# Eight sums of the out projection's weight, beside the first columns of the second half's input projection instead of beside that half's local attention

## The chip, the cores and the metric

The kernel runs on one core of a Trainium2 chip. The metric is device time in microseconds: 2577.95 us before the change, the median of three runs (2577.09 to 2580.97). The chip has other cores, and nothing runs on them here. The engines are called as in the profile: PE (matrix multiplication) with PEld (its weight loads), DVE (vector), ACT (scalar), POOL (GpSimd), and SP, which only issues transfers here. Each engine takes its own instructions strictly in the order of its queue.

## What is computed

One layer of a sequence model over 2048 tokens of width 1024, in float32:

```python
u = rms_norm(h, g_mix_pre)
z = u @ w_in                                   # 1024 x 2816
ya = swa_with_sinks(qa, ka, va, sinks)         # local attention, 8 heads of 64
yh = hgrn2(qh, fh, ih, gh, lb, onorm)          # gated linear recurrence, 4 heads of 128
y = concatenate([ya, yh]) @ w_out              # the out projection
h = h + rms_norm(y, g_mix_post)
...                                            # cross attention, then a SwiGLU block
```

The change touches only when four combinations of the blocks of `w_out` (1024 x 1024) are computed. It changes no value.

## The kernel before, in words

**Precision.** A float32 product is made of three fast products: each operand is split into a rounded high part (`hi`) and the rest (`lo`), and PE multiplies high by high, high by low and low by high (`mm3`, lines 166 to 168; `products`, lines 1047 to 1049). The split of a 128x1024 tile costs one pass of POOL or ACT for `hi` (line 146 or 148) and one of DVE for `lo` (line 149).

**Seven products for eight.** The large products are done in 2x2 blocks with seven block products (Strassen's scheme in Winograd's form). The side that stays in memory, here the weight, is needed in seven forms: three of its four blocks as they are, and four combinations of blocks, called 5, 7, 6 and 4 in the code. With blocks a(i,j) of the weight these are, each made from the one before: 5 = a(0,1) - a(0,0), 7 = a(1,1) - a(0,1), 6 = 7 + a(0,0), 4 = a(1,0) - 6.

**Where the combinations of `w_out` are made.** `combined` (lines 951 to 971) makes them ahead of time, in two halves of 128x1024 elements each, and so issues eight sums. One sum is: the load of one or two tiles of `w_out` on SP's queue (line 75; tile `x`), three steps of waiting (`yield`), one `TENSOR_TENSOR` of DVE (line 958, `x<-x,x`), the store of the result to the DRAM tensor `w_s` on SP's queue (line 78), and one more `yield`. A half takes 16 steps of the generator. The blocks a(0,j) are loaded in two transfers of 64 partitions each, the blocks a(1,j) in one. In all that is 20 loads (16 of 256 KB, 4 of 512 KB), 8 sums and 8 stores of 512 KB. Much later the out projection loads `w_s` and splits it (lines 911 and 914).

The tag `x` has three buffers. It is also the tile of the decays of the input projection (line 652: `e1`), once for each of four pairs of columns, and of the folded weights of the cross attention later.

**The stages around the change** (`mix`, lines 202 to 270). First comes the input projection of tokens 0 to 1023 in seven-product form (`in_first`). Then a stage of four interleaved generators:

- `in_proj(1, u)`, called `cols`: the input projection of tokens 1024 to 2047, column by column. A column has 128 outputs; its weights are loaded (tile `raw`, three buffers) and split (`whi`, `wlo`), and PE multiplies 2 x 24 products of 128x512. The first step takes two columns (keys and values of the local attention), each later one takes one; there are 21 steps.
- `swa(range(8))`: local attention of the first half, one step for each 128 tokens, and one more.
- `hgrn(range(8))`: the recurrence of the first half.
- `swa(range(8, 16))`: local attention of the second half.

The order of the text is: two steps of `cols`; then per step of the first half's local attention five steps of the recurrence and one of `cols`; then per step of the second half's local attention one step of `cols` and, from the second on, four steps of the sums, which is one sum. The last sum stands beside the last step.

**What sets the real order.** The text only gives a priority. A scheduler, run when the program is built, walks through a model of the engines and gives each engine, whenever it comes free, the first instruction in the order of the text whose inputs and buffers are there. So a load whose buffer is free is put early in SP's queue, whatever the text has beside it. The result is one fixed queue for each engine. On the chip an instruction at the head of a queue that waits holds up all behind it.

`mark` (lines 982 to 987) notes the last ACT and DVE instruction of the text so far, and `behind` (lines 974 to 980) makes the DVE sums of line 958 stand behind it in DVE's queue. Loads and stores are not bound by it.

**Memory.** The pools of this stage reuse the room of those of `in_first`. As the pools are laid out, one of the three `x` buffers lies in room that no tile had before; the two others lie where the tile `pair` of the last load `pair<-un_d` was. Its last reader is the split of that tile by DVE (line 914, `u<-pair`).

Of the kernel before, what the change touches and what calls it, by code (L numbers as in the profile page):

```python
# [28 lines left out]
NPB = TB // P  # L29
NT = T // P  # L30
# [18 lines left out]
class Layer:  # L49
# [152 lines left out]
    def mix(self):  # L202
        tc, I = self.tc, self.I
        kw = dict(reuse_waits="tile")
        with contextlib.ExitStack() as left:
            def pool(name, at, **k):
                return at.enter_context(tc.tile_pool(name=name, bufs=1, **k, **kw))

            self.mc = pool("mc", left)
            self.r_x = self.cst.tile([P, NT], F32, name="r_x")  # L210
            with (
                tc.tile_pool(name="t1", bufs=3, **kw) as self.ts,
                tc.tile_pool(name="t2", bufs=3, **kw) as self.tb,
                tc.tile_pool(name="s1", bufs=2, side="right", **kw) as self.st_pool,
                contextlib.ExitStack() as at,
            ):
                self.banks(at, "ps1", **MOST)
                self.raws, self.parts, self.sums = 3, 3, 3
                u = self.in_first()
            self.banks(left, "ps2", **FOUR)  # L220
            self.hg = pool("hg", left)
            self.wp = pool("wp", left)
            self.io = pool("io", left)
            with tc.tile_pool(name="sw", bufs=1, side="right", **kw) as self.sw:
                self.zero_tiles()
                swa = self.swa(range(NPB), "st")
                hgrn = self.hgrn(range(NPB), "h")
                cols = self.in_proj(1, u)
                for _ in range(2):
                    next(cols)  # L230
                for _ in swa:
                    for _ in range(5):
                        next(hgrn)
                    next(cols)
                for _ in hgrn:
                    pass
                jobs = self.jobs()
                sums = self.w_sums()
                swa = self.swa(range(NPB, NT), "sth")
                for i, _ in enumerate(swa):  # L240
                    next(cols)
                    if i:
                        self.mark()
                        for _ in range(4):
                            next(sums, None)
                for _ in cols:
                    pass
                for _ in sums:
                    pass
            phases = self.phases(jobs, None, lambda: self.io_tile("z"))  # L250
            with tc.tile_pool(name="xp", bufs=1, side="right", **kw) as self.xp:
                fold = self.fold_cross()
                for i, _ in enumerate(self.hgrn(range(NPB, NT), "gt")):
                    for _ in range(1 if i % 5 else 0):
                        next(fold)
                for _ in range(8):
                    next(phases)
                for _ in fold:
                    pass
            left.close()  # L260
            with (
                tc.tile_pool(name="t3", bufs=3, **kw) as self.ts,
                tc.tile_pool(name="t4", bufs=3, **kw) as self.tb,
                tc.tile_pool(name="s3", bufs=2, side="right", **kw) as self.st_pool,
                contextlib.ExitStack() as at,
            ):
                self.banks(at, "ps3", **MOST)
                self.raws, self.parts, self.sums = 6, 4, 5
                for _ in phases:
                    pass  # L270
# [1437 lines left out]
```

## Time and profile before

| what | value |
|---|---|
| median of three runs | 2577.95 us |
| the profiled execution's own time | 2576.83 us |
| its span, first to last instruction | 2574.7 us |
| granted TensorE clock, mean | 0.995 |
| stage of the change, roughly | 260 to 660 us of the span |
| sums of line 958, first and last start | 524.2 and 636.7 us |
| first load of `w_out` for them | 504.2 us |
| first and last store to `w_s` | 525.5 and 638.0 us |
| first load of `w_s` by the out projection | 664.8 us |

In the rows that follow, `x` and a number in brackets is a count of instructions; in the table by windows each engine's busy time in microseconds stands ahead of its count, then the granted clock of PE, the mean busy share of the 16 DMA engines, and GB/s. Times on a timeline are microseconds from the start of the span, followed by the duration; `[4.91 <-DMA x<-in_w_out_dram]` says that the engine stood idle for 4.91 us before the instruction and what ended that.

### The profile page before, as it was taken

How to read it: one execution, taken by the hardware profiler on the slowest of the kernel's cores; microseconds unless marked ns; L12 is line 12 of the kernel's file. 1: busy time of each engine (PE TensorE's matmuls, PEld its weight loads, DVE VectorE, ACT ScalarE, POOL GpSimd, SP SyncE). 2: the span in 40 equal slices, each digit the busy share in tenths (PEclk: the TensorE clock that was granted, in tenths of full speed). 3: DMA queues.
4: the chain of work that ended last, by engine and by line, in shares of the span. 5: the costliest groups of instructions: out<-in, count | busy, mean ns of one | idle time of the engine just before them, and what ended most of it. 6: DMA issues, size and time to landing. Idle time of an engine off the chain costs nothing.

```text
span 2574.7 us, 34494 instructions
## 1 busy us (share of the span) xinstructions
PE 2518.1 (98%) x12160; PEld 2108.6 (82%) x12160; DVE 1747.3 (68%) x2781; ACT 1262.3 (49%) x2641; POOL 481.6 (19%) x651
## 2 busy tenths in 40 slices
PE   7989999999999999999999999999999999999998
PEld 6878788878997888888788888888888888888786
DVE  7675578778666668697776665575666566664756
ACT  5453366656555575565564333353333334543443
POOL 4240334321321334224210000000000000000022
PEclk9999999999999999999999999999999999999999
DMA  5335655484896787767983542253555434576798
GB/s 188 135 119 180 198 159 153 150 259 169 251 331 236 229 273 218 246 229 207 314 264 123 171 163 83 82 196 123 180 200 193 158 128 142 191 220 185 224 222 211
DMA packets 285389, 495.78 MB, mean 193 GB/s; under 512 B 20640, under 2 KB 143520, under 8 KB 285216
## 3 DMA queue, kind: packets, MB, share of 16 engines
q1 hardware_dynamic: 272256, 446.38, 51.5%
q0 software_dynamic: 10656, 38.80, 8.1%
q10 hardware_dynamic: 2304, 8.39, 0.8%
q8 instruction: 96, 1.57, 0.3%
q14 instruction: 77, 0.63, 0.1%
HBM read 326.78 MB, written 166.72 MB: 192 GB/s over the span
## 4 chain that ended last, share of the span: by engine, by line
PE 86%; DMA 5%; DVE 4%; issue 2%; POOL 2%; ACT 1%; SPq 0%; DVEq 0%; POOLq 0%; ACTq 0%
PE psm L1047 23%; PE psm L1049 23%; PE psm L1048 23%; PE psg L168 2%; PE psg L166 2%; PE psg L167 2%; PE pss L1299 2%; DMA pair<-in_x_dram 1%; PE pss L167 0%; PE psh L168 0%; PE psh L167 0%; PE pss L168 0%; PE pss L166 0%; PE psh L166 0%; DMA qd<-z_d 0%
## 5 line engine op out<-in xcount | busy, mean ns | idle before, releaser
L1047 PE MATMUL psm<-T,S 128*128 128x512 f32 x2664 | 1032.7, 392 | 14.9 <-ACT part L1062 8.6
L1048 PE MATMUL psm<-T,S 128*128 128x512 f32 x2664 | 1039.5, 390 | 0.0
L1049 PE MATMUL psm<-T,S 128*128 128x512 f32 x2664 | 1033.6, 391 | 2.2 <-DVE S L914 2.2
L1047 PEld LDWEIGHTS psm<-T,S 128*128 128x128 f32 x2664 | 501.1, 188 | 121.9 <-ACT part L1062 10.5
L1049 PEld LDWEIGHTS psm<-T,S 128*128 128x128 f32 x2664 | 500.9, 188 | 108.2 <-DVE S L914 4.4
L1048 PEld LDWEIGHTS psm<-T,S 128*128 128x128 f32 x2664 | 501.2, 188 | 102.6
L911 ACT ACTIVATE S<-sum 128x512 fp32r<-128x512 f32 (+1 forms) x338 | 207.9, 619 | 329.6 <-PE psm L1049 320.5
L914 DVE TENSOR_TENSOR S<-sraw,S 128x512 fp32r<-128x512 f32 (+1 forms) x311 | 214.8, 698 | 220.6 <-ACT S L911 208.3
L914 DVE TENSOR_TENSOR S<-sum,S 128x512 fp32r<-128x512 f32 (+1 forms) x404 | 277.1, 691 | 79.9 <-ACT S L911 67.0
L1062 ACT ACTIVATE part<-psm 128x512 f32<-128x512 f32 x297 | 175.3, 592 | 188.9 <-PE psm L1049 180.5
L911 ACT ACTIVATE S<-sraw 128x512 fp32r<-128x512 f32 (+1 forms) x272 | 166.4, 617 | 143.3 <-PE psm L1049 137.6
L1417 POOL DMA_DIRECT2D row<-y_d x28 | 25.0, 892 | 1071.4 <-DMA sraw<-hid_d 905.3
L1388 ACT ACTIVATE junk<-row 128x512 f32<-128x512 f32 x160 | 99.6, 624 | 95.3 <-DVE row L1410 34.6
L914 DVE TENSOR_TENSOR T<-row,T 128x1024 fp32r<-128x1024 f32 x104 | 123.3, 1193 | 29.6 <-ACT T L911 29.3
L166 PE MATMUL psg<-u,whi 128*128 128x512 f32 x352 | 141.8, 403 | 1.0 <-POOL whi L148 1.0
L168 PE MATMUL psg<-u,wlo 128*128 128x512 f32 x352 | 140.2, 398 | 1.5 <-DVE wlo L149 1.5
L167 PE MATMUL psg<-u,whi 128*128 128x512 f32 x352 | 140.1, 398 | 0.0
L911 ACT ACTIVATE T<-row 128x1024 fp32r<-128x1024 f32 x104 | 105.6, 1026 | 24.7 <-DMA row<-in_w_down_dram 11.8
L913 POOL TENSOR_SCALAR S<-sum 128x512 fp32r<-128x512 f32 x66 | 51.9, 787 | 217.8 <-PE psm L1049 138.6
L1592 DVE TENSOR_TENSOR part<-psm,part 128x512 f32<-128x512 f32 x66 | 45.5, 689 | 66.5 <-PE psm L1049 66.4
L149 DVE TENSOR_TENSOR wlo<-raw,whi 128x1024 fp32r<-128x1024 f32 x54 | 68.8, 1274 | 27.6 <-ACT whi L146 18.9
L1583 DVE TENSOR_TENSOR row<-psm,part 128x512 f32<-128x512 f32 x66 | 45.5, 690 | 56.0 <-PE psm L1049 55.7
(331 smaller groups left out, 3659.2 us busy)
## 6 DMA issues: line engine op xcount, KB each, us to landing
sraw<-in_w_gate_dram SPq DMA_DIRECT2D x44, 512.0 KB, 4.9
sraw<-in_w_up_dram SPq DMA_DIRECT2D x44, 512.0 KB, 4.8
hid_d<-row SPq DMA_DIRECT2D x44, 512.0 KB, 2.7
h_d<-row SPq DMA_DIRECT2D x32, 512.0 KB, 6.9
y_d<-row SPq DMA_DIRECT2D x32, 512.0 KB, 3.8
sraw<-hid_d SPq DMA_DIRECT2D x32, 512.0 KB, 5.2
row<-h_d POOLq DMA_DIRECT2D x30, 512.0 KB, 7.7
row<-y_d POOLq DMA_DIRECT2D x28, 512.0 KB, 7.2
```

Of the source, the lines that this page charges most:

```text
L149: nc.vector.tensor_tensor(lo, raw, f32(hi), ALU.subtract)
L166: nc.tensor.matmul(ps, ah, bh, start=(i == 0), stop=False)
L167: nc.tensor.matmul(ps, ah, bl, start=False, stop=False)
L168: nc.tensor.matmul(ps, al, bh, start=False, stop=(i == n - 1))
L911: self.nc.scalar.activation(hi, raw, AF.Copy)
L913: self.nc.gpsimd.tensor_scalar(hi, raw, 1.0, 1.0, ALU.mult, ALU.mult)
L914: self.nc.vector.tensor_tensor(lo, raw, f32(hi), ALU.subtract)
L1047: nc.tensor.matmul(ps, s[:, 0, k, :], t[:, 0, k, :], start=st, stop=False, **kw)
L1048: nc.tensor.matmul(ps, s[:, 0, k, :], t[:, 1, k, :], start=False, stop=False, **kw)
L1049: nc.tensor.matmul(ps, s[:, 1, k, :], t[:, 0, k, :], start=False, stop=sp, **kw)
L1062: nc.scalar.activation(t, ps, AF.Copy)
L1388: self.nc.scalar.activation(junk, a, AF.Square, scale=float(D) ** -0.5, accum_out=to)
```

## The change

The creation of the sums' generator (and of `jobs`, which issues nothing by itself) moves ahead of the two first steps of `cols`. Each of these two steps is now followed by 16 steps of the sums, which is one whole half, four sums. The loop over the second half's local attention loses its sums.

```diff
                 cols = self.in_proj(1, u)
+                jobs = self.jobs()
+                sums = self.w_sums()
                 for _ in range(2):
                     next(cols)
+                    self.mark()
+                    for _ in range(16):
+                        next(sums, None)
+                for _ in sums:
+                    pass
                 for _ in swa:
                     for _ in range(5):
                         next(hgrn)
                     next(cols)
                 for _ in hgrn:
                     pass
-                jobs = self.jobs()
-                sums = self.w_sums()
-                swa = self.swa(range(NPB, NT), "sth")
-                for i, _ in enumerate(swa):
+                for _ in self.swa(range(NPB, NT), "sth"):
                     next(cols)
-                    if i:
-                        self.mark()
-                        for _ in range(4):
-                            next(sums, None)
                 for _ in cols:
-                    pass
-                for _ in sums:
                     pass
```

The same 20 loads, 8 sums and 8 stores are issued, by the same engines and queues. In the text they stand ahead of all local attention and all of the recurrence, behind three of the 22 columns. The `mark` of the first four sums now names the second column's last instructions, that of the last four the third column's.

## The prediction

> **What bounds the kernel now.** The page comes first: its span, its engine totals and the chain that ended last.
>
> ```profile
> span 2574.7 us, 34494 instructions
> PE 2518.1 (98%) x12160; PEld 2108.6 (82%) x12160; DVE 1747.3 (68%) x2781; ACT 1262.3 (49%) x2641; POOL 481.6 (19%) x651
> PE 86%; DMA 5%; DVE 4%; issue 2%; POOL 2%; ACT 1%; SPq 0%; DVEq 0%; POOLq 0%; ACTq 0%
> ```
>
> PE is busy for 98% of the span, 2574.7 - 2518.1 = 56.6 us short of all of it. The change adds and removes no matmul, so it can only win or lose pieces of such idle time. The next question is where they lie. The table by windows of 10 us answers it (columns: PE, PEld, DVE, ACT, POOL, clock, DMA share, GB/s); first the place that the sums go to, then the place that they leave, then the seam to the next stage.
>
> ```profile
> 260.00:270.00 10.00, 6.99 (x25) 4.82 (x24) 9.27 (x11) 5.55 (x7) 5.85 (x6) 0.90 0.88 279
> 270.00:280.00 10.00, 10.00 (x43) 8.24 (x43) 6.70 (x10) 0.91 (x3) 8.61 (x8) 0.93 0.92 314
> 280.00:290.00 10.00, 10.00 (x45) 8.26 (x45) 3.03 (x4) 2.41 (x4) 1.81 (x2) 1.00 0.53 155
> 290.00:300.00 10.00, 10.00 (x46) 8.27 (x45) 1.23 (x1) 1.20 (x2) 1.05 (x1) 1.00 0.47 167
> 300.00:310.00 10.00, 10.00 (x57) 8.68 (x56) 5.73 (x26) 5.61 (x23) 2.37 (x3) 1.00 0.50 154
> 310.00:320.00 10.00, 10.00 (x60) 8.74 (x59) 5.15 (x18) 2.64 (x7) 3.88 (x7) 1.00 0.62 184
> 320.00:330.00 10.00, 10.00 (x52) 8.42 (x52) 9.31 (x25) 7.32 (x25) 3.21 (x6) 1.00 0.42 135
> ...
> 530.00:540.00 10.00, 9.52 (x48) 7.69 (x46) 4.89 (x9) 3.25 (x9) 2.05 (x3) 1.00 1.06 302
> 540.00:550.00 10.00, 7.91 (x38) 6.00 (x39) 9.09 (x24) 5.17 (x15) 6.05 (x9) 1.00 0.93 299
> 550.00:560.00 10.00, 8.11 (x47) 6.76 (x46) 6.60 (x16) 3.37 (x10) 1.26 (x2) 1.00 1.05 310
> ...
> 650.00:660.00 10.00, 7.18 (x37) 5.91 (x37) 7.34 (x12) 4.20 (x9) 2.12 (x3) 0.85 1.02 329
> 660.00:670.00 10.00, 9.09 (x71) 8.64 (x71) 6.49 (x12) 6.88 (x19) 6.27 (x7) 0.97 1.04 295
> ```
>
> Three windows beside the sums, 530 to 560, lose 0.48 + 2.09 + 1.89 = 4.46 us of PE, with the DMA engines full. From 270 to 330 PE loses nothing, and between 280 and 300 DVE is all but idle. The seam at 650 to 670 loses 2.82 + 0.91 = 3.73 us.
>
> Is the loss at 530 to 560 caused by the sums? The view of the tile `x` over 500 to 640 us, the timeline of DVE, and that of PE say so:
>
> ```profile
> L75 SPq DMA_DIRECT2D x<-in_w_out_dram x20: 390/606/1635, 504.2 to 604.2; - x20
> L958 DVE TENSOR_TENSOR x<-x,x x8: 1210/1226/1239, 524.2 to 636.7; 128x1024 f32<-128x1024 f32 x8
> L78 SPq DMA_DIRECT2D w_s<-x x8: 320/334/490, 525.5 to 638.0; - x8
>   DMA x<-in_w_out_dram: 4.9, 1
>   issue: 3.4, 1
>   DMA w_s<-x: 0.9, 1
> ```
>
> ```profile
> 536.63 1.23 DVE L958 TENSOR_TENSOR x<-x,x 128x1024 f32<-128x1024 f32 x1 [4.91 <-DMA x<-in_w_out_dram]
> 543.39 1.23 DVE L958 TENSOR_TENSOR x<-x,x 128x1024 f32<-128x1024 f32 x1 [0.85 <-DMA w_s<-x]
> 557.18 1.23 DVE L958 TENSOR_TENSOR x<-x,x 128x1024 f32<-128x1024 f32 x1 [3.36 <-issue]
> ```
>
> ```profile
> 540.59 0.66 PE L760 MATMUL pss<-ident,S 128*128 128x128 f32 x4 [1.07 <-DVE w_mn L731]
> 547.93 0.50 PE L769 MATMUL psh<-pth,vst 128*128 128x512 f32 x1 [1.19 <-ACT pth L764]
> 558.82 0.63 PE L760 MATMUL pss<-ident,S 128*128 128x128 f32 x4 [1.90 <-DVE vst L712]
> ```
>
> A sum stands at the head of DVE's queue and waits for its load or for a buffer; the local attention's DVE work behind it is late; PE waits 1.07, 1.19 and 1.90 us for that work or what follows from it. The three waits of the sums add to 9.1 us, of which about half reaches PE.
>
> **The change part by part.** *Taken away from 504 to 638 us:* 20 loads, 8 sums (8 x 1.226 = 9.8 us of DVE) and 8 stores. DVE and SP have no say of their own in the end here; what the path gets back is the 4.46 us of PE. Bounds: 0, if another wait steps in (a `qd` load that is late anyway), and 4.46 from those windows. I take the upper end: PE reads 10.00 in the windows on both sides where DVE isn't held by a sum. What is late next there is the local attention's own chain, which the rows of 270 to 330 show to be covered in the first half by the same kind of columns.
>
> *Put at 260 to 350 us:* the same 48 instructions. On DVE the sums stand behind the split of the second and third column, and PE has those columns' products to do meanwhile:
>
> ```profile
> 269.73 2.06 DVE L149 TENSOR_TENSOR wlo<-raw,whi 128x1024 fp32r<-128x1024 f32 x1
> 271.71 2.06 DVE L914 TENSOR_TENSOR u<-pair,u 128x1024 fp32r<-128x1024 f32 x1
> 273.69 1.63 DVE L149 TENSOR_TENSOR wlo<-raw,whi 128x1024 fp32r<-128x1024 f32 x1
> 287.27 1.23 DVE L149 TENSOR_TENSOR wlo<-raw,whi 128x1024 fp32r<-128x1024 f32 x1 [1.06 <-POOL whi L148]
> ...
> 303.19 0.35 DVE L731 CUSTOM_DVE_ANT_0 S<-pst,wmask,nsink 128x128 f32<-128x128 f32 x1 [9.19 <-PE pst L727]
> ```
>
> Two of the three `x` buffers come free when the last `u<-pair` ends (271.71 + 2.06 = 273.8). No sum can run before one of them is loaded, and by then the three columns are split (273.69 + 1.63 = 275.3). Their 3 x 48 = 144 products at 45 to 46 per 10 us keep PE for about 32 us, to near 298. DVE's first work for the local attention is at 303.19, where DVE, not PE, has waited 9.19 us. So the first sums fall into a time in which nobody waits for DVE.
>
> Not all eight do. The DMA view gives their transfers:
>
> ```profile
> x<-in_w_out_dram SPq DMA_DIRECT2D x16, 256.0 KB, 6.4
> x<-in_w_out_dram SPq DMA_DIRECT2D x4, 512.0 KB, 5.9
> w_s<-x SPq DMA_DIRECT2D x8, 512.0 KB, 4.7
> qd<-z_d SPq DMA_DIRECT2D x64, 128.0 KB, 3.3
> ```
>
> 16 x 256 + 4 x 512 + 8 x 512 KB are 10.5 MB, 34 us of all DMA engines at the 302 to 314 GB/s of the full windows. The share left free from 270 to 330 is 0.08 + 0.47 + 0.53 + 0.50 + 0.38 + 0.58 = 2.54 windows, 25 us. So the sums end near 350, and about a third of them stand beside the first local attention of the first half, with the DMA engines as full as at 530 to 560. Bounds of their cost there: 0, as in the full window 270 to 280, and 4.46 us in 30 us over the 50 us from 300 to 350, 7.4 us. I take 1.5 us: the rate of 0.149 us per us over one window, 320 to 330, the only one of the six after 270 whose DVE is nearly full (9.31), since a held DVE harms only where it has no slack.
>
> The Trainium skill speaks against this change at this point (page DMA: Bandwidth & Descriptors, section "Issuing engines are not separate DMA queues"): all transfers end on the same 16 DMA engines and interleave there, whichever engine issued them. By it the sums' bytes crowd the loads of whatever stage they are put in. The trace agrees with the rule where it shows it, with a share of 1.06, 0.93 and 1.05 at 530 to 560. By it alone the sum would be the first rival's, below.
>
> *SP's queue.* The 28 issues move past all loads of the first half's local attention and recurrence; a store waits for its sum, a load for its buffer, and behind each stand loads of `qd`, `kr`, `raw`. At 0.3 to 0.6 us an issue they are about 14 us of SP over 80 us, no bound. What such a wait can do is the second rival.
>
> *The earliest load.* One `x` buffer lies in unused room, so its first 512 KB may be loaded far ahead, as the gain of the memory tokens was:
>
> ```profile
> L75 SPq DMA_DIRECT2D g<-in_g_mem_dram x1: 328/328/328, 161.7 to 161.7; - x1
> ```
>
> It was loaded at 161.7 us, as its buffer came free, for work near 580. Such a load costs 0 to 1.7 us (0.52 MB at 302 GB/s) if it crowds the start of the kernel; I take 0, by the nearest row: in the window 270 to 280, at a DMA share of 0.92, PE loses nothing.
>
> *The seam.* It may win all of its 3.73 us or lose as much again; the instructions there are the same, so I take 0.
>
> **Sum.** -4.46 + 1.5 = -2.96 us on the profiled execution, whose own time is 2576.83 us with a span of 2574.7: 2573.9. The median of the runs is 1.12 us above that execution: 2577.95 - 2.96 = **2575.0 us**.
>
> **The rivals.**
>
> *The crowd only moves.* The sums cost at 300 to 350 what they cost at 530 to 560, 4.46 us: 2577.95 us. For it speaks the sum of bytes; against it DVE's slack. This is also the case in which the change doesn't do what it says: the text sets a priority only, and if the scheduler puts most sums behind 300 us, they stand beside a local attention again.
>
> *Slower, by SP's and DVE's queues in the first half.* Each sum that reaches the head of DVE's queue too early holds DVE, and its store holds SP, as at 536.63, for 4.91 us. DVE's idle time from 280 to 320 is 6.97 + 8.77 + 4.27 + 4.85 = 24.9 us; less 9.8 us for the sums, 15.1 us are left as cover. N such waits cost PE 4.91 N - 15.1 us: nothing up to 3, 4.5 us with 4, 14.4 us with 6. The kernel is slower by over 0.2% (5.16 us) from six on: 2577.95 - 4.46 + 14.4 = 2587.9 us. Against it: of the eight sums before, only three waited, 9.1 us in all, less than the cover. For it: three buffers and eight sums that now follow one another at once, each waiting for the store of an earlier one.
>
> *Faster, the seam too.* With DVE free of 9.8 us and the DMA engines of 10.5 MB, the scheduler can bring work of the next stage forward, and the 3.73 us at the seam go as well, with no cost early: 2577.95 - 4.46 - 3.73 = 2569.8 us. Against it: the seam's windows have a DMA share of 1.02 and 1.04 from their own loads.
>
> **How the numbers follow.** Forecast 0.45, own range 2572 to 2577.5; crowd moves 0.25; slower 0.15; seam too 0.15. A measurement of this kernel can tell about 0.2% from no change, 5.16 us: faster means below 2572.8, slower above 2583.1. The forecast gives 0.08 to faster (its lower end) and 0.37 to the same; the moved crowd 0.22 to the same and 0.03 to slower (its upper bound of 7.4 us with a loss at the seam); the two other rivals go to their sides. Faster 0.23, same 0.59, slower 0.18. The range goes from 2569, below the seam case, to 2584, above the moved crowd with its upper bounds (-4.46 + 7.4 + 1.7 + 1.5); what is left out is most of the slower rival and a little below.
>
> **What would show it.** Right: line 958 runs between 278 and 350 us and is gone from 504 to 638; the three windows at 530 to 560 read 10.00 for PE with a DMA share near 0.6; PE loses 1 to 2 us from 300 to 350. Wrong: PE's losses at 300 to 350 of 4 us or more (crowd moves), waits of DVE for `x<-in_w_out_dram` above 15 us in all (slower), PE still short at 530 to 560 (the sums were not its cause), or a seam that differs from 3.73 us by more than 3.

## The result and the profile after

The changed kernel takes 2590.55 us, median of five runs (2587.45 to 2594.72), beside 2578.13 us for the kernel before in the same session (2577.09 to 2581.78). The ratio is 1.0046, with a 95% interval from 1.0035 to 1.0057: slower by 0.46%, or 12.4 us, and above the predicted range. The profiled execution took 2592.66 us. The ratios in this document are of fast runs alone, and one slow run, of 3617.9 us in the experiment e10, is left out of them. Line numbers of the changed kernel behind line 250 are two lower than those of before: the sums are L956, the tile `qs` L689 and L690.

The page of the changed kernel, its span, engine totals and chain:

```profile
span 2591.0 us, 34492 instructions
PE 2525.5 (97%) x12160; PEld 2114.0 (82%) x12160; DVE 1754.0 (68%) x2781; ACT 1262.6 (49%) x2641; POOL 474.7 (18%) x651
PE 76%; DMA 8%; DVE 6%; issue 5%; POOL 3%; ACT 2%; SPq 0%; POOLq 0%; DVEq 0%; ACTq 0%
```

PE does the same 12160 products, is idle for 2591.0 - 2525.5 = 65.5 us (before 56.6), and is busy for 7.4 us longer with the same products; a lower granted clock, seen below, is part of that. In the chain DMA rises from 5% to 8%. Where the loss lies is seen in windows of 50 us (columns as in the prediction; the last three are clock, DMA share, GB/s), first of the changed kernel, then of the kernel before:

```profile
300.00:350.00 50.00, 45.55 (x256) 39.70 (x254) 35.54 (x95) 22.88 (x80) 17.84 (x25) 0.97 1.05 303
400.00:450.00 50.00, 47.05 (x268) 40.69 (x267) 40.95 (x93) 31.73 (x94) 21.77 (x30) 0.97 0.55 161
500.00:550.00 50.00, 49.56 (x263) 41.93 (x262) 37.65 (x100) 29.37 (x85) 20.24 (x30) 1.00 0.49 154
550.00:600.00 50.00, 49.23 (x257) 41.18 (x257) 42.71 (x116) 32.70 (x94) 14.93 (x24) 1.00 0.52 163
650.00:700.00 50.00, 44.97 (x325) 42.44 (x325) 31.67 (x43) 27.02 (x56) 11.77 (x13) 0.97 0.79 237
700.00:750.00 50.00, 46.62 (x383) 45.47 (x383) 30.53 (x45) 27.61 (x74) 22.24 (x26) 1.00 0.91 298
750.00:800.00 50.00, 49.43 (x346) 45.50 (x344) 26.31 (x33) 26.17 (x53) 2.40 (x4) 1.00 0.86 305
800.00:850.00 50.00, 47.24 (x204) 38.13 (x205) 37.37 (x49) 27.07 (x50) 10.44 (x14) 1.00 0.63 213
sum 550.00, PE 528.88 PEld 463.42 DVE 402.42 ACT 318.37 POOL 162.15; mean PE 48.08 PEld 42.13 DVE 36.58 ACT 28.94 POOL 14.74
```

```profile
300.00:350.00 50.00, 50.00 (x288) 43.46 (x287) 35.12 (x108) 28.29 (x97) 18.45 (x27) 1.00 0.54 163
400.00:450.00 50.00, 49.36 (x289) 42.59 (x287) 42.51 (x98) 31.49 (x93) 20.98 (x32) 1.00 0.51 150
500.00:550.00 50.00, 47.42 (x240) 38.93 (x239) 42.40 (x102) 28.92 (x79) 20.88 (x29) 1.00 0.76 224
550.00:600.00 50.00, 48.10 (x258) 40.72 (x257) 41.08 (x110) 29.45 (x85) 11.21 (x21) 1.00 0.76 242
650.00:700.00 50.00, 46.27 (x360) 44.55 (x360) 34.40 (x48) 29.70 (x70) 18.49 (x20) 0.97 0.90 283
700.00:750.00 50.00, 50.00 (x425) 50.00 (x424) 33.73 (x49) 30.02 (x77) 19.63 (x21) 1.00 0.98 346
750.00:800.00 50.00, 46.57 (x274) 40.00 (x274) 25.13 (x32) 26.11 (x47) 3.04 (x4) 1.00 0.86 291
800.00:850.00 50.00, 50.00 (x226) 41.47 (x225) 39.90 (x51) 25.48 (x53) 15.56 (x22) 1.00 0.59 174
sum 550.00, PE 537.38 PEld 470.52 DVE 409.78 ACT 323.08 POOL 170.42; mean PE 48.85 PEld 42.77 DVE 37.25 ACT 29.37 POOL 15.49
```

The sums (300 to 850 us, eleven windows, three of them not shown) say that PE is busy for 537.38 - 528.88 = 8.50 us less. 4.45 us of it are lost at 300 to 350, and the clock of 0.97 there takes another 0.03 x 50 = 1.5 us. At 400 to 450 it is 2.31 us more than before, and at 650 to 850 4.58 us more. At 500 to 600, the place that the sums left, 3.27 us are won.

Not all of this stands beside the sums. The last sum starts at 335.9 us, and none of their work runs at 400 to 450. PE's longest wait there is one of 1.91 us at 414.64 us, for DVE (`w_mn`), and the clock of 0.97 takes another 1.5 us. So close to 4 us are lost some 70 us behind the last sum.

The place that the sums went to, in 10 us, and inside it in 2 us:

```profile
300.00:310.00 10.00, 10.00 (x59) 8.67 (x58) 7.65 (x28) 6.07 (x25) 3.92 (x6) 1.00 1.03 346
310.00:320.00 10.00, 7.36 (x39) 6.12 (x37) 2.95 (x6) 0.94 (x2) 2.32 (x3) 1.00 1.12 284
320.00:330.00 10.00, 8.19 (x38) 7.43 (x39) 8.35 (x21) 5.12 (x16) 3.47 (x4) 0.83 1.07 302
330.00:340.00 10.00, 10.00 (x59) 8.58 (x58) 8.97 (x23) 5.61 (x16) 1.29 (x3) 1.00 1.13 304
```

```profile
318.00:320.00 2.00, 0.00 (x0) 0.00 (x0) 0.00 (x0) 0.00 (x0) 0.00 (x0) 1.00 1.00 276
320.00:322.00 2.00, 0.19 (x1) 0.19 (x2) 0.90 (x2) 1.34 (x4) 0.00 (x0) 0.95 1.03 383
322.00:324.00 2.00, 2.00 (x10) 2.00 (x11) 2.00 (x11) 1.69 (x7) 0.16 (x1) 0.50 1.11 250
324.00:326.00 2.00, 2.00 (x8) 1.84 (x8) 1.59 (x3) 0.68 (x3) 1.58 (x3) 0.70 1.18 272
```

From 318 to 320 us no engine does anything; only the DMA engines work, at a share of 1.00. The timelines of DVE, ACT and PE name what they wait for:

```profile
313.48 1.23 DVE L956 TENSOR_TENSOR x<-x,x 128x1024 f32<-128x1024 f32 x1 [4.95 <-DMA x<-in_w_out_dram]
320.40 0.63 ACT L689 ACTIVATE qs<-qd 128x512 fp32r<-128x512 f32 x1 [9.32 <-DMA qd<-z_d]
321.06 0.69 DVE L690 SCALAR_TENSOR_TENSOR qs<-qd,qs 64x512 fp32r<-64x512 f32 x1 [4.53 <-ACT qs L689]
321.81 0.58 PE L724 MATMUL pst<-kh,qs 128*128 128x256 f32 x1 [4.45 <-DVE qs L690]
```

Read from the bottom: PE waits 4.45 us for `qs`, DVE for ACT, ACT 9.32 us for the load of `qd`. The stretch ends with a transfer, not with the sum that held DVE for 4.95 us shortly before. The view of the tile `qd` from 268 to 345 us gives the same for all such loads, in the kernel before and in the changed one:

```profile
  DMA qd<-z_d: 6.3, 3
DMA to landing us min/median/max: 2.7/3.6/6.4
```

```profile
  DMA qd<-z_d: 20.4, 4
DMA to landing us min/median/max: 4.0/5.8/8.6
```

ACT sits idle for these loads for 20.4 us in place of 6.3, and a load takes 5.8 us to land in place of 3.6 (medians).

The slower landing isn't the whole delay. The load of `qd` that ends the stall also goes out late. Here is its issue on SP's queue, in the kernel before and in the changed one:

```profile
307.13 1.24 SPq L75 DMA_DIRECT2D qd<-z_d  x2
310.73 2.19 SPq L75 DMA_DIRECT2D qd<-z_d  x2
```

In the kernel before it goes out 0.1 us after DVE has read the tile's last contents (until 307.02 us). In the changed kernel DVE is done with them at 305.82 us, and the load goes out 4.9 us later. In that stretch SP had just waited 3.0 us with a load of `w_out` whose buffer a store to `w_s` was still reading, and it issued two more loads of `w_out` ahead of `qd`. ACT starts on the tile at 320.40 us in place of 314.02. Of these 6.4 us, 3.6 are the later issue and 2.8 the longer time from issue to use.

The view of the tile `x` has the sums themselves:

```profile
L75 SPq DMA_DIRECT2D x<-in_w_out_dram x20: 426/604/922, 274.5 to 328.1; - x20
L956 DVE TENSOR_TENSOR x<-x,x x8: 1224/1225/1791, 282.9 to 335.9; 128x1024 f32<-128x1024 f32 x8
  DMA x<-in_w_out_dram: 12.8, 6
  DMA w_s<-x: 2.8, 2
```

All 20 loads go out in 54 us, where before they took 100 (504.2 to 604.2).

### The profile page after: what moved, and what is told of

The parts are those of the page before. It is cut to its first block, busy times and chain, and to the rows that moved or that the text cites. A ratio compares the mean times of both kernels' runs of the same rounds, so it can differ in the third digit from the quotient of the medians.

```text
span 2591.0 us, 34492 instructions
## 1 busy us (share of the span) xinstructions
PE 2525.5 (97%) x12160; PEld 2114.0 (82%) x12160; DVE 1754.0 (68%) x2781; ACT 1262.6 (49%) x2641; POOL 474.7 (18%) x651
## 4 chain that ended last, share of the span: by engine, by line
PE 76%; DMA 8%; DVE 6%; issue 5%; POOL 3%; ACT 2%; SPq 0%; POOLq 0%; DVEq 0%; ACTq 0%
PE psm L1045 21%; PE psm L1047 21%; PE psm L1046 21%; PE psg L168 2%; PE psg L166 2%; PE psg L167 2%; PE pss L1297 1%; DMA row<-y_d 1%; DMA row<-h_d 1%; DVE S L912 1%; DMA z<-in_w_out_dram 1%; DMA kk<-z_d 1%; DMA sraw<-in_w_in_dram 1%; DMA y_d<-row 1%; DMA qk_s<-qs 0%
## 5 line engine op out<-in xcount | busy, mean ns | idle before, releaser
L1590 DVE TENSOR_TENSOR part<-psm,part 128x512 f32<-128x512 f32 x66 | 45.4, 688 | 65.6 <-PE psm L1047 65.5
```

## The experiments

All ratios are to the kernel before on the same chip, with the 95% interval. They are worked out from all the runs, and can differ by some hundredths of a per cent from the quotient of two medians. In the expectations VectorE is DVE, ScalarE is ACT and SyncE is SP. The theories changed as the results came: A and B first, then H (a sum that waits for its load holds VectorE) against C (the bytes crowd the DMA engines), then Q (the loads of `w_out` stand ahead of others in SyncE's queue) against C.

### First group: is it the place of the sums at all?

**No sums (e1).** `sums = iter(())`, and the out projection's first job reads `I["w_out"].rearrange(...)` in place of `w_s`.

> Leaves the eight sums, their loads and stores out; the out projection reads rows of the plain weight in their place, so the output isn't the reference's. Theory A (the sums' place carries all of it: where they stand they hold DVE and crowd the transfers, and that lateness carries on): without them the time is that of before less the 4.5 us lost at 530 to 560, 2573 to 2574 us, and no other place of the stage loses more than in before. Theory B (the place itself is worth about +3 us, 5.8 lost early for 3 won late, and the rest of the +12 us is the new order that the scheduler gives to every queue of the stage): the time can lie anywhere from 2569 to 2585, and PE has losses of 2 us and more at places where before has none, without any sum.

Measured: 2576.95 us, 0.9997 (0.9985 to 1.0008). So in the kernel before, all the sums with all their transfers cost nothing that can be measured: leaving them out wins between 3.9 us and -2.1 us. The windows beside their old place show what became of the idle PE there:

```profile
500.00:550.00 50.00, 48.38 (x247) 40.49 (x246) 41.49 (x106) 30.30 (x82) 18.93 (x30) 0.97 0.45 136
550.00:600.00 50.00, 50.00 (x261) 42.24 (x260) 38.52 (x100) 29.67 (x82) 11.63 (x20) 1.00 0.51 161
sum 550.00, PE 538.57 PEld 470.74 DVE 403.76 ACT 323.96 POOL 167.55; mean PE 48.96 PEld 42.79 DVE 36.71 ACT 29.45 POOL 15.23
```

Without any sum, with a DMA share of 0.45, PE still loses 1.62 us at 500 to 550, and over the eleven windows it is busy for only 538.57 - 537.38 = 1.19 us more than before. The clock of 0.97 in the first row takes 1.5 us that the kernel before didn't lose there (1.00). So 2.86 us of PE are won at 500 to 600, and other places and the clock take them back.

**One sum per step of the first half's local attention (e2, and e17, the same program again).**

```python
for i, _ in enumerate(swa):
    ...
    if i:
        self.mark()
        for _ in range(4):
            next(sums, None)
```

> All eight sums beside the first half's local attention, one for each step, not eight at once. Theory A: the early crowd is thinned, so PE loses at most 2 us beside them and the time is 2574 to 2578 us. Theory B: it's a new order again; the time scatters by about 5 us around 2580 whatever stands where, with losses of PE away from the sums.

> The sums spread over the steps of the first half's local attention once more, in more rounds. If the sums cost nothing in the kernel before (the kernel without sums: 0.9997), nothing can be won by a place for them: within 0.1% of before. If the 4.46 us term of the prediction exists after all: 0.998.

Measured: 0.9992 (0.9981 to 1.0003) and 0.9989 (0.9978 to 1.0000). The 20 loads are spread from 278.1 to 478.2 us. This earlier place costs nothing that can be measured. Both suggest a gain of 0.1%. By itself neither shows it, and taken together their interval only just leaves out 1, by less than the 0.07% that chance gives below (e4).

**Four sums early, four late (e3), and six early (e12, run with the third group).** `range(8)` and `range(12)` in place of `range(16)`, the rest in the old place.

> Four sums early (two behind each of the first two steps of columns), four beside the second half's local attention. Theory A: half of the early cost and less of the late one, 2579 to 2584 us, between the two kernels, with half the loss at 300 to 340 (about 3 us). Theory B: not ordered by the number of early sums; outside 2578 to 2590 as likely as inside.

> Six of the eight sums early (three behind each of the first two column steps), two in the old place. Four early gave 1.0006, eight 1.0046. Straight line between: 1.0026. C with a cover that ends between four and eight: 1.001 to 1.003. If the loss needs all eight: within 0.1% of before.

Measured: 1.0006 (0.9996 to 1.0016) with four and 1.0033 (1.0020 to 1.0046) with six. It isn't a straight line through zero, which would put four sums at 0.23%: the first four cost nothing that can be measured, and not the half of the loss (about 3 us of PE) that was expected of them. Six cost a little more than was expected by a cover (1.001 to 1.003) or by a line from four to eight (1.0026), and the interval leaves room for both. With four, the windows at 310 to 320 read

```profile
310.00:320.00 10.00, 9.02 (x52) 7.68 (x50) 5.25 (x16) 2.41 (x7) 3.65 (x6) 1.00 0.43 128
```

and with six

```profile
310.00:320.00 10.00, 8.50 (x46) 7.07 (x44) 2.56 (x6) 1.20 (x2) 2.53 (x4) 1.00 1.05 298
320.00:330.00 10.00, 7.27 (x35) 6.64 (x36) 7.03 (x17) 4.65 (x16) 2.98 (x4) 0.83 1.09 322
```

With four the transfers are through by 310 us (share 0.43). With six they run on beside the first local attention, and PE loses 4.23 us in these two windows.

**A lag of one step (e4).** `if True:` and `range(4 if i else 3)` in the old place.

> The sums stay beside the second half's local attention, but each is marked one step behind its loads, so that DVE should not stand before a load that hasn't landed. Theory A: the waits of DVE for x (9.1 us in before) fall below 3 us, the 4.5 us of PE at 530 to 560 go, 2573 to 2575 us. Theory B: those waits fall too, but the time is before's plus or minus 5 us by the new order.

Measured: 1.0007 (0.9997 to 1.0017). The scheduler gave this text the same operations in the same order on all five engines' queues as the kernel before. So it tells nothing of the lag, but it is a measurement of an unchanged program: 0.07% is what chance gives here.

Theory B, that a new order of work alone scatters the time by several tenths of a per cent, isn't borne out: e1, e2 and e3 are all new orders, and all within 0.1%.

### Second group: load, sum or crowd?

**The change again (e5).**

> The change once more, with the line numbers of the kernel before. Theory H (the hold): a sum that stands at the head of VectorE's queue holds it until its load lands (4.95 us at 313.48 us in the changed kernel's trace), and the local attention of the first half behind it starts late. Theory C (the crowd): the 10.5 MB of the sums hold the DMA engines at a share of 1.03 or more from 280 to 340 us, so that loads of the running stages land late. Both: 1.0046 of the time of before again, within 0.001, with a PE loss of 5 to 7 us between 310 and 330 us. A third, that the loss is only an accident of one measurement: within 0.1% of before.

Measured: 2591.27 us, 1.0046 (1.0032 to 1.0060). PE loses 1.10 + 3.39 = 4.49 us from 310 to 330:

```profile
310.00:320.00 10.00, 8.90 (x48) 7.42 (x46) 3.02 (x7) 1.40 (x3) 2.67 (x5) 1.00 1.09 284
320.00:330.00 10.00, 6.61 (x29) 6.07 (x30) 6.04 (x16) 3.71 (x13) 2.56 (x4) 0.83 1.09 289
```

It repeats, in the same place (4.45 us in the first profile), somewhat less than the 5 to 7 us expected.

**Sums and stores without loads (e6).** The sums read a constant tile `c2`, and no tile of `w_out` is loaded.

> The early place with all eight sums and their eight stores, but each sum made from a constant tile in place of the 20 loads of w_out (the sums' values are left out of the computation). What is left are 9.8 us of VectorE and 4.2 of 10.5 MB. H: no sum waits for a load, so nothing is held: within 0.1% of before, no PE loss at 310 to 330 us. C: 40% of the bytes, 1.0018 of the time of before.

Measured: 0.9999 (0.9989 to 1.0008). VectorE's 9.8 us and the 4.2 MB of stores are hidden. C by bytes alone, which asked for 1.0018, is outside the interval. One thing limits this run: without loads to wait for, the sums run from 277.4 to 293.2 us, ahead of the first local attention, and not from 282.9 to 335.9 as in the change. What the sums and stores would cost at 300 to 335 without loads isn't shown by it.

**Loads without sums and stores (e7).** `made` does nothing for `w_s`.

> The early place with the 20 loads alone: no sums, no stores, the out projection reads rows of the plain w_out in their place (the sums are left out of the computation). H: nothing on VectorE waits for these loads: within 0.1% of before. C: 60% of the bytes in a shorter time: 1.003 to 1.0046 of the time of before.

Measured: 1.0030 (1.0021 to 1.0039). Against H in its pure form: VectorE has no sum to be held by. Here are the windows of e7 and, under them, the waits of the tile `qd`:

```profile
300.00:350.00 50.00, 44.46 (x237) 38.81 (x236) 26.01 (x85) 23.21 (x80) 14.45 (x22) 0.93 0.78 217
```

```profile
  DMA qd<-z_d: 27.3, 4
```

PE loses 5.54 us at 300 to 350, and the clock of 0.93 takes 3.5 us more. ACT waits 27.3 us for `qd`. The loads alone make a stall, with no sum and no store. Such a wait of ACT is no price by itself: it is 13.1 us in the same stretch of e2, which costs nothing. And here too the load goes out late: the second pair of `qd` is issued at 294.63 us in place of 281.32, 6.5 us after its buffer is free, behind loads of `w_out`.

**The bunch in the old half (e8).** `if i == 1:` and `range(32)` in the old place.

> The old half, but all eight sums in one bunch behind the second step of the second half's local attention. If the bunch is the cause, whether by H or by C, the loss of the change appears there as well: 1.003 to 1.005 of the time of before, with PE losses of 5 us or more in the 40 us beside the sums. If it is the early place (the first local attention and the columns' splits beside it): within 0.1% of before.

Measured: 1.0025 (1.0015 to 1.0035), with the 20 loads in 65 us (502.8 to 567.6). So a bunch costs there too, though less. The place expected for it was wrong: the three windows from 530 to 560 lose 1.93 + 1.85 + 0.38 = 4.16 us, no more than the 4.46 of before. The clock of 0.83 at 540 to 550 takes 1.7 us that before had not (1.00); the rest of the loss is not traced to one place.

```profile
530.00:540.00 10.00, 8.07 (x36) 6.29 (x34) 3.38 (x7) 2.23 (x7) 1.94 (x2) 1.00 1.10 249
540.00:550.00 10.00, 8.15 (x33) 6.39 (x34) 9.94 (x25) 5.18 (x15) 5.66 (x8) 0.83 0.97 303
550.00:560.00 10.00, 9.62 (x52) 8.00 (x52) 6.75 (x16) 3.17 (x10) 1.81 (x3) 1.00 0.97 289
```

### Third group: bytes or the place in a queue?

**Loads alone, half their columns (e9), and a quarter (e13, run with the fourth group).** `dst[:, :, 0:256], src[:, :, 0:256]` and `0:128` for the loads of `w_out`. The two have the same operations in the same order on every queue.

> As the run with the 20 early loads alone (1.0030), each load with half its columns: 3.15 of 6.3 MB, the same issues and buffers (the sums are left out of the computation). Theory C, the crowd with a cover: what fits into the free share of the DMA engines costs nothing, so half the bytes land without loss: within 0.1% of before. C without a cover, loss by bytes: 1.0015. Theory Q, that the issues themselves and their order in SyncE's queue cost: 1.003 again.

> As the run with 20 early loads of half the columns (1.0021), now of a quarter (1.6 of 6.3 MB), with the same order of instructions on every queue (the sums are left out of the computation). Theory Q (SyncE's queue holds 15 loads of w_out between the first two loads of qd): 1.0015 to 1.0021 again, qd of the second half of that first step issued only near 290 us. Theory C (bytes on the DMA engines): half the loss or less, 1.0000 to 1.0010.

Measured: 1.0021 (1.0012 to 1.0029) and 1.0008 (0.9998 to 1.0017). With all bytes it was 1.0030. From all to a quarter the loss falls by more than the intervals allow for chance; from all to half it doesn't, and the run with all bytes has another order in its queues. The cover that C was given (no loss with half) isn't there. But a late place in the queue is there as well. With half the columns SP's timeline has

```profile
279.72 9.28 SPq L75 DMA_DIRECT2D x<-in_w_out_dram  x12
292.73 0.59 SPq L75 DMA_DIRECT2D qd<-z_d  x1
```

where in the kernel before the same load of `qd` had gone out by 277.08 us (a pair in 1.35 us from 275.73), and the DMA engines are not full while PE stalls:

```profile
300.00:310.00 10.00, 5.91 (x31) 5.05 (x31) 3.52 (x13) 1.84 (x6) 2.16 (x2) 0.87 0.58 173
```

So Q is real as a delay. With half the bytes `qd` lands in 4.0 us (median), hardly later than the 3.6 of before, so this run's loss goes with the late issue rather than with slow landing. The quarter has the same order in the queue, and the same load goes out at 289.57 us, near 290 as Q said; its loss is 0.08%, at most 0.17%. That bounds the price of a delay of 13 us, and not of the 16 us with half the bytes: SP waits at a load of `w_out` until the buffer's earlier load has landed, so fewer bytes also shorten the queue's delay. Bytes and queue aren't fully parted by these two runs.

**Loads alone on ScalarE's queue (e10).** `self.nc.scalar.dma_start` for the loads of `w_out`.

> As the run with the 20 early loads alone (1.0030), these loads issued on ScalarE's DMA queue in place of SyncE's; all bytes (the sums are left out of the computation). Q: the loads of qd and kr no longer stand behind a load of w_out that waits for its buffer, so within 0.1% of before. C: the same 16 DMA engines carry the same bytes, 1.002 to 1.004, with ScalarE still waiting over 15 us for qd at 285 to 330 us.

Measured: 1.0036 (1.0021 to 1.0050). Freeing SyncE's queue doesn't help. It isn't a clean test: ScalarE is now held by these loads (its waits for `qd` ahead of `qs` are 13.6 us, not over 15; one more of 8.2 us, ahead of a copy of `z`, is put down to `qd` too). The Trainium skill says of this (page DMA: Bandwidth & Descriptors, section "Issuing engines are not separate DMA queues") that all transfers share the same 16 DMA engines, whichever engine issues them; the 1.0036 agrees.

**Loads and sums, no stores (e11).** The sums as in the change; `self.store(...)` left out for `w_s`.

> Early loads and the eight sums on VectorE, no stores; the out projection reads rows of the plain w_out (the sums' results are left out of the computation). If VectorE's hold by a sum that waits for its load adds to the crowd (H on top of C): 1.0038 to 1.0046. If the hold lies beside the lateness that the loads make anyway: 1.003 as with the loads alone, and the rest of the change's 1.0046 is in the stores and in the order of work that the scheduler sets with them.

Measured: 1.0048 (1.0035 to 1.0060). Beside loads alone that is 0.18% more, just outside what the two intervals allow together (0.15%). The sums that wait for their loads are the likely reason; the two runs also have different orders in their queues. The window of e11:

```profile
300.00:350.00 50.00, 43.48 (x225) 37.23 (x224) 27.52 (x76) 20.17 (x71) 13.07 (x20) 0.90 0.82 207
```

PE loses 6.52 us, and the clock of 0.90 takes 5.0 us: 11.5 us, the whole of what the kernel is slower by (0.48% of 2578 is 12.4 us).

### Fourth group: take `qd` out of the queue

**`qd` on ScalarE's queue, before (e14) and with the change (e15).** `self.put(qd[0:64], qsrc)` and the same for `qd[64:128]`.

> Control: the kernel before with the loads of qd issued on ScalarE's queue in place of SyncE's. By Q and C alike about the time of before, 0.999 to 1.003: ScalarE gets 128 issues of 0.1 to 0.6 us and their waits.

> The whole change, with the loads of qd on ScalarE's queue: no load of w_out stands ahead of them any more. Q: the loss against its control (e14) falls from 0.46% to under 0.2%. C: it stays at 0.3% or more, since the same bytes are on the same 16 engines.

Measured: 1.0019 (1.0008 to 1.0030) for the control, 1.0056 (1.0041 to 1.0070) with the change. The change costs 1.0056 / 1.0019 = 1.0037 with `qd` off SyncE's queue; the two intervals together give 0.2 to 0.55%. Q asked for under 0.2%, so it is only just left out. The loads of `qd` land in 6.0 us in e15 and 3.7 us in its control (medians, 268 to 345 us), as C says. But ScalarE's queue isn't free either: one half of the load that ends a stall of 6.91 us of PE goes out at 314.59 us, after two waits of ACT of 2.96 and 2.94 us for other work. The 64 loads of `qd` are half of the 128 issues that were expected.

**The bunch behind the first step of the first half's local attention (e16).**

```python
if not i:
    self.mark()
    for _ in sums:
        pass
```

> All eight sums in one bunch, but behind the first step of the first half's local attention in the text, so that the first loads of qd, kr and vr stand ahead of them in SyncE's queue. Q: only the later steps' loads are held, 1.000 to 1.003. C: the bunch's bytes are the same, 1.003 to 1.0046.

Measured: 1.0046 (1.0032 to 1.0060). The first loads of `qd`, `kr` and `vr` go ahead of the bunch, and the loss is the same as with the change. So a late first load isn't what decides. Later loads of `qd` still stand behind loads of `w_out` here, as in the change.

No version was found that is clearly faster than the kernel before, and by e1 there is little to find: even leaving the sums out wins nothing that can be measured.

## Why the prediction was wrong, step by step

- **Taken away from 504 to 638 us, -4.46 us: the size was wrong, and it was all of the gain.** "I take the upper end" was the choice. The waits of the sums at 530 to 560 were real, and in the changed kernel most of that idle time is gone (3.27 us at 500 to 600). But e1 shows that the kernel doesn't get it back in the end (1.19 us of PE over 550 us, no measurable time). The lower bound of that step, 0, was the right end. In the changed kernel 4.58 us more are lost at 650 to 850.
- **Put at 260 to 350 us, 1.5 us: this is the step that failed.** The bounds were 0 to 7.4 us, and I took the rate of one window, 320 to 330, "since a held DVE harms only where it has no slack". The changed kernel loses 4.45 us of PE and 1.5 us of clock there, 6.0 us in place of 1.5. The step asked for DVE's slack, and what ended the idle time was a load of `qd`: e6 keeps DVE's work (at an earlier time) and costs nothing, e7 has no work on DVE and costs 0.30%. That the free share of the DMA engines was 2.54 windows was counted rightly, and that the transfers would run past 330 followed from it; what such a share does to loads that others wait for was not priced.
- **The cover was right for the first half of the bunch.** Four sums cost nothing that can be measured (e3), as the products of the columns hide what is late until about 310 us. Six are not (e12).
- **The earliest load and the seam, 0 each, and what stands between.** No step had the loss at 400 to 450 either: 2.31 us of PE and 1.5 us of clock, some 70 us behind the last sum. The first load went out at 274.5 us, so it crowded nothing earlier. At 650 to 700 PE loses 5.03 us in place of 3.73. The later windows, 700 to 850, lose 6.71 in place of 3.43, which no step had. e11 is as slow as the change and loses only 0.38 us of PE at 400 to 450, with another order of the queues there than the change has; which of the later losses come from the new order and which from lateness stays open.
- **SP's queue, no bound.** This term was put at nothing by the issue times alone, and that was too little. In the changed kernel the load of `qd` that ends the stall goes out 4.9 us after its buffer is free. In e13, where a load of `qd` goes out 13 us late and the bytes are few, the loss is 0.08% (at most 0.17%); the share of such a delay in the changed kernel stays open.
- **The rivals.** The crowd that only moves gave 2577.95 us and was wrong, since the crowd had cost nothing where it was. The slower rival had the right sign and side, 2587.9 us, but its formula was about holds of DVE: the measured waits of 12.8 + 2.8 = 15.6 us exceed its cover of 15.1 by 0.5 us, and the kernel lost 12.4. Eight waits came, of 2.0 us each and not of 4.91, so that its number came near is luck. Loads without any sum make 0.30% (e7), and with the sums it is 0.18% more (e11).
- **The signs named.** PE's loss at 300 to 350 was above 4 us, as named for a crowd that costs. The waits for `x<-in_w_out_dram` were 12.8 us, under the 15 named for the slower rival, which shows that this sign was tied to the wrong resource. The sums ran from 282.9 to 335.9 us, as the forecast had it.

What is shown: most of the cost comes with the bunch of loads. 20 loads in 54 us (the change) or 65 us (e8) cost 0.46% and 0.25%; in 100 us (before) or 200 us (e2) they cost nothing. It doesn't need the sums or the stores (e7), it is smaller with a quarter of the bytes (0.08% in e13 against 0.30% in e7), and it stays when the loads of `w_out` or of `qd` move to another queue or the first loads of `qd` go first (e10, e15, e16). What is open: how much of it is slow landing and how much late issue, since loads that land slowly also hold SP's queue; whether the waiting sums themselves add the 0.18% of e11; and why PE loses time at 400 to 450 and behind 650.

## What to carry to other kernels

Idle time of the bounding engine beside some work isn't what that work costs: a run that leaves the work out prices it, and only such a price can be won by moving it. Work that is free while its transfers are spread can cost when they are bunched, because loads that others wait for then go out and land late; so count the DMA share of the new place over the time that the bunch takes, and look for the small loads there that are used as soon as they land. An engine's slack says nothing about that.

## What the runs showed of the hardware

A stall of PE costs more than its idle time. In the changed kernel PE is idle for 4.45 us until 321.81 us, and the granted clock is 0.95, 0.50 and 0.70 in the three windows of 2 us behind 320 us: (0.05 + 0.50 + 0.30) x 2 = 1.7 us on top. With e11 it is 5.0 us on top of 6.52. The Trainium skill has this (page TensorE: Matmul & The Clock Gate, section "Why this matters for your kernels"): a gap of more than about 3 us in PE's work brings the clock down to half. The 0.50 agrees. But here the gap needn't be that long: behind the wait of 1.91 us at 414.64 us, with two of 0.45 and 0.60 us close behind it, the granted clock is 0.50 at 418 to 420 us. And a wait of 1.90 us in the kernel before, at 558.82 us, leaves it at 1.00.

A load of 128 KB (`qd`) took 5.8 us to land (median) in the changed kernel, where the DMA engines had a share of 1.05 at 300 to 350 us, and 3.6 us before, where it was 0.54; the issue of a load of `w_out` took 0.604 us of SP (median), so 20 of them are 12 us of that queue.
